# Taking the norm of the sample's block apart: scaling ahead of the first products, transposes between gate's and up's

## The chip, the core and the metric

The kernel runs on one core of a Trainium2 chip. A core has a matrix engine (TensorE, in the profile PE, with its weight loads as PEld) and three engines for element-wise work: VectorE (DVE), ScalarE (ACT) and GpSimd (POOL). SyncE (SP) issues most transfers. Each engine works its instructions off in the order in which they were put into its queue; an instruction that waits holds up all that stand behind it. The metric is the device time of one execution in microseconds. The kernel before takes 1778.29 us, the median of three runs (1778.0 to 1786.5).

## The reference

One inference step of a small two-layer network for two groups of tokens: a prompt of 512 rows and a sample of 8 x 16 = 128 rows, each row 1024 wide, in float32. Layer 0 has a mixer of two kinds of attention, layer 1 a banded softmax attention; after each mixer comes the same feed-forward part (FFN):

```python
def _rmsnorm(x, g):
    y = xf * lax.rsqrt(jnp.mean(xf * xf, axis=-1, keepdims=True) + EPS)
    return (y * g.astype(jnp.float32)).astype(x.dtype)

def _swiglu(h, wg, wu, wd):
    return (jax.nn.silu(h @ wg) * (h @ wu)) @ wd

xp = xp + _swiglu(_rmsnorm(xp, norm_ffn_g[layer]), w_ffn_gate[layer], w_ffn_up[layer], w_ffn_down[layer])
xs = xs + _swiglu(_rmsnorm(xs, norm_ffn_g[layer]), w_ffn_gate[layer], w_ffn_up[layer], w_ffn_down[layer])
```

The hidden width of the FFN is 2816. The change touches only how the norm of the sample's rows is fitted into the start of each of the two FFNs.

## The kernel before

Prompt and sample are handled together as 640 rows in five blocks of 128; block 4 is the sample. Weights in float32 are split into a high part (`wh`, a rounded copy made by ACT, line 289) and a low part (`wl`, the rest, made by DVE, line 290), and each product is three matmuls: high by high, high by low, low by high (lines 692 to 694). There are four buffers each for `wh` and `wl`, so splits run up to four products ahead.

**The norm of a block** is `norm_block` (line 247). `rstd_of` (line 230) forms the reciprocal root: ACT squares both halves of the rows and sums them (`sqj`, line 235), DVE adds (`rv`, 240), ACT takes logarithm and exponential (`rr`, 241 and 242), DVE does a correction step (`ra`, 243, and `rr`, 244). Then each half of the rows is scaled into a tile `h` (line 252), the first half by DVE, the second by POOL; PE transposes it in four pieces into a bank of PSUM (`tp`, line 255); and ACT and DVE in turn bring the eight pieces into the transposed input `fT`, multiplied by the norm's weight (lines 261 and 263).

**The FFN** (`ffn`, line 738) takes the columns of the 640 rows in two halves of 320: the first is prompt only, the second holds the rest of the prompt and the sample. Its weights gate and up are worked through in pairs of 128 columns; each pair of columns of one matrix is an entry of `mats` with four functions. `part(0)` and `part(1)` are the plain products with the first and the second half of the rows; each makes four products of 12 matmuls, 48 in all, into two tiles `pb`. `head`, `body` and `tail` are a form with seven products in place of eight (tiles `py`, `px`, `pq`), which needs sums of weights (`sw`, made by POOL at line 699) and sums of the input (`comb`, DVE at line 657, tiles `xs`). `block` splits a part of the input into high (`xb`, `xt`, ACT at line 664) and low (DVE at line 665). The blocks `b11` and `b21` cover the first half of the rows, `b12` and `b22` the second; `t1` to `t4` are those of the sums.

The first entries of gate and up are done by plain products, since the sample's rows come last: they are complete only when `out_sample` has added its product to them (line 626), right ahead of the FFN. The order in the program is: blocks b11 and b21, `part(0)` of gate, `part(0)` of up, the norm of block 4, blocks b12 and b22, `part(1)` of gate, `part(1)` of up, `head` of the next pair, the sums and blocks t1 to t4, and then the pairs' bodies:

```python
block("b11")
block("b21")
part(0)
last_norm(mats[1][3](0))
block("b12", gt_)
```

`part(0)` returns its last matmul. What `last_norm` gets is the last matmul of up's first half; the transposes are bound to be issued behind it (`tc.issue_after`, line 253).

The queues' order is made by a planner that goes by the program's order (an earlier statement has priority), by when operands are ready in its own estimate, and by the free buffers of each tag. The tag `ws` has six buffers; the tiles `sqj`, `h`, the results `sg` of gate and `up` of up, and `xs` share it. The plain products' tiles `pb` and the transposes' `tp` share five banks of PSUM.

Of the kernel before, what the change touches and what calls it, by code (L numbers as in the profile page):

```python
# [13 lines left out]
ALU = mybir.AluOpType  # L14
PSUM = bass.MemoryType.PSUM

P = 128
# [38 lines left out]
def kernel(  # L56
# [8 lines left out]
    nc = tc.nc  # L65
# [27 lines left out]
    @contextmanager  # L93
    def ffn_pools():
        with tc.tile_pool(name="ffn", bufs=1, reuse_waits="tile") as m:
            pools["stage"] = m
            with tc.tile_pool(name="pf", bufs=5, space=PSUM, reuse_waits="tile") as a:
                banks.update(za=a, zb=a)
                yield

    def tagged(tag, bufs, where="all"):
        def f(shape, name, dt=F32):
            return pools[where].tile(shape, dt, tag=tag, bufs=bufs, name=name)
        return f
# [5 lines left out]
    ws = tagged("ws", NWS)  # L110
# [108 lines left out]
        fill=0.0, base=DS - 1, channel_multiplier=-1,  # L219
    )  # L220

    xs_flat = x_sample.rearrange("b t d -> (b t) d")

    def x_rows(src_p, src_s, b):
        return src_p[0, b * P:(b + 1) * P, :] if b < 4 else src_s
# [4 lines left out]
    def rstd_of(xt, sb=None):  # L230

        ss = small.tile([P, 2], F32, tag="ss", name="ss")
        for i in range(2):
            j = (sb or ws)([P, 512], "sqj")
            nc.scalar.activation(j, xt[i], AF.Square, scale=1.0 / 32.0, accum_out=ss[:, i:i + 1])
        v = small.tile([P, 1], F32, tag="rv", name="rv")
        r = small.tile([P, 1], F32, tag="rr", name="rr")
        a = small.tile([P, 1], F32, tag="ra", name="ra")
        V = nc.vector
        V.tensor_scalar(v, ss[:, 0:1], ss[:, 1:2], EPS, op0=ALU.add, op1=ALU.add)  # L240
        nc.scalar.activation(r, v, AF.Ln)
        last_exp[:] = [nc.scalar.activation(r, r, AF.Exp, scale=-0.5)]
        V.tensor_scalar(a, r, r, v, op0=ALU.mult, op1=ALU.mult)
        V.tensor_scalar(r, a, -3.0, r, op0=ALU.add, op1=ALU.mult)
        return r

    def norm_block(xt, gi, hT, b, sb=None, bank=None, after=None):
        r = rstd_of(xt, sb)
        for i in range(2):
            tp = (bank or za)([P, 4, P], "tp")  # L250
            h = (sb or ws)([P, 512], "h")
            scaled = (nc.vector, nc.gpsimd)[i].tensor_scalar(h, xt[i], r, -0.5, op0=ALU.mult, op1=ALU.mult)
            with tc.issue_after(after.ins) if after else nullcontext():
                for j in range(4):
                    nc.tensor.transpose(tp[:, j, :], h[:, j * P:(j + 1) * P], ident)
            for j in range(4):
                c = 4 * i + j
                if len(hT) == 4:
                    d = hT[c // 2][:, c % 2, b * P:(b + 1) * P]
                    if j % 2:  # L260
                        nc.vector.tensor_scalar(d, tp[:, j, :], gm[:, gi, c:c + 1], None, op0=ALU.mult)
                    else:
                        nc.scalar.activation(d, tp[:, j, :], AF.Copy, scale=gm[:, gi, c:c + 1])
                    continue
                H = hT[c][:, 0, b * P:(b + 1) * P]
                L = hT[c][:, 1, b * P:(b + 1) * P]
                g = gm[:, gi, c:c + 1]
                nc.scalar.activation(H, tp[:, j, :], AF.Copy, scale=g)
                nc.vector.scalar_tensor_tensor(
                    L, tp[:, j, :], g, H.bitcast(F32), op0=ALU.mult, op1=ALU.subtract)  # L270
        return scaled

    def new_hT(nm):
        return [t5([P, 2, NT], f"{nm}{c}", F32R) for c in range(8)]

    def new_fT(nm):

        return [t5([P, 2, NT], f"{nm}{c}") for c in range(4)]
# [459 lines left out]
    def ffn(l, xt, fT, after, last_norm):  # L738
        X, comb, block = operand(fT)
        c0, silu = 0, []  # L740
        for gi, G in enumerate(GROUPS):
            gT, mats = [], []
            for c in range(c0, c0 + G, 2):
                gt = [(t5 if gi % 2 == 0 and c == c0 else gt_)([P, 2, NT], "gT", F32R) for _ in range(2)]
                gT += gt
                sg = [ws([P, 2, 320], "sg") for _ in range(2)]

                def out_g(m, n, a, b, sg=sg, done=[0, 0]):
                    if b is None:
                        nc.scalar.copy(sg[m][:, n, :], a)  # L750
                    else:
                        nc.vector.tensor_add(sg[m][:, n, :], a, b)
                    done[m] += 1
                    if done[m] == 2:

                        with tc.issue_after(last_exp[0].ins):
                            silu.append(nc.scalar.activation(sg[m], sg[m], AF.Silu))

                def out_u(m, n, a, b, sg=sg, gt=gt, up=[None, None]):
                    if up[m] is None:  # L760
                        up[m] = ws([P, 2, 320], "up")
                    if b is None:
                        nc.scalar.copy(up[m][:, n, :], a)
                    else:
                        nc.vector.tensor_add(up[m][:, n, :], a, b)
                    if b is None and n == 0:
                        return
                    g = gt[m].rearrange("p i (n t) -> p i n t", n=2)
                    for i in range(2) if b is None else (n,):
                        s = sg[m][:, i, :]  # L770
                        nc.vector.tensor_mul(s, s, up[m][:, i, :])
                        nc.scalar.copy(g[:, 0, i, :], s)
                        nc.vector.tensor_sub(g[:, 1, i, :], s, g[:, 0, i, :].bitcast(F32))
                for w, o in ((w_ffn_gate, out_g), (w_ffn_up, out_u)):
                    mats.append(fast_pair(w[l], c * P, X, o))
            for i, (head, body, tail, part) in enumerate(mats):
                if gi == 0 and i == 1:
                    continue
                if gi == 0 and i == 0:


                    block("b11")
                    block("b21")
                    part(0)
                    last_norm(mats[1][3](0))
                    block("b12", gt_)
                    block("b22")
                    part(1)
                    mats[1][3](1)
                    mats[2][0]()  # L790
                    comb("t3", "b22", "b12")
                    block("t3")
                    comb("t1", "b12", "b11")
                    comb("t2", "b22", "t1")
                    block("t2")
                    block("t1")
                    comb("t4", "b21", "t2")
                    block("t4")
                    continue
                if gi or i > 2:  # L800
                    head()
                if i > 2 * (gi == 0):
                    mats[i - 1][2]()
                body()
            mats[-1][2]()
            if gi == len(GROUPS) - 1:
                with tc.issue_after(silu[-1].ins):
                    nc.scalar.preload_act_table_set(LOGSET)
            for half in range(2):
                last = half == 1 and gi == len(GROUPS) - 1  # L810

                def ev(b, ps):
                    nc.vector.tensor_add(xt[b][half], xt[b][half], ps)
                proj_as(l, w_ffn_down[l][c0 * P:(c0 + G) * P, :], 512 * half, 512, gT, ev,
                        tail=TAIL if last else 1, after=after if last else None)
            c0 += G
# [11 lines left out]
    hT = new_hT("hTa")  # L828
# [266 lines left out]
    for t in ORDER.split():  # L1095
        step(t)
    hT = new_fT("fT0")
    xt = mixer_end(w_out_ab[0], oT, oS, lambda b: x_rows(x_prompt, xs_flat, b), 1, hT, a_sample,
                   [FIRST + 99500 + 1000 * t for t in WHEN[0]])
# [9 lines left out]
        last_scaled[:] = [norm_block(xt[b], 2, hT2, b)]  # L1109
    stack.close()  # L1110
    with ffn_pools():
        ffn(0, xt, hT, after0, lambda mm: norm_block(xt[4], 1, hT, 4, after=mm))
    hT = hT2


# [53 lines left out]
    for half in range(2):  # L1169
# [7 lines left out]
        for p in range(p0 + 1, p0 + 4):  # L1177
            c_attend(p, *c_pair(p))

    hT = new_fT("fT1")  # L1180
    xt = mixer_end(w_out_c[0], oT, oS, lambda b: xd[b], 3, hT, lambda: (mixer_banks(*BANKS[2]), [c_sample(h) for h in range(2)]),
                   [FIRST + 299500 + 1000 * t for t in WHEN[1]])
# [11 lines left out]
        nc.sync.dma_start(dst, y)  # L1194
    stack.close()
    with ffn_pools():
        ffn(1, xt, hT, after1, lambda mm: norm_block(xt[4], 3, hT, 4, after=mm))


# [37 lines left out]
```

## Time and profile before

| | |
|---|---|
| median of three runs | 1778.29 us |
| profiled execution: its own time | 1781.72 us |
| profiled execution: span | 1780.0 us |
| granted TensorE clock, mean | 0.979 |
| busy: PE / PEld | 95% / 86% |
| busy: DVE / ACT / POOL | 62% / 46% / 18% |
| chain that ended last: PE / DVE / ACT | 82% / 11% / 3% |

The profile is of one execution. The page gives busy time per engine, the span in 40 slices, the chain of waits that ended last, and groups of instructions by line. A row of a timeline gives the start in us from the span's start, the duration, the engine, the line, the operation, `out<-in`, the shape, how many instructions were merged, and in brackets how long the engine had been idle and which instruction ended that. A row of the table of stretches gives, for each stretch, its length, each engine's busy time with the number of instructions, the granted clock, and the transfers' share and rate. FFN 0 begins at about 440 us, FFN 1 at about 1321 us.

### The profile page before, as it was taken

The page shows a single profiled execution, that of the slowest core. Times are in us where ns is not written, and L with a number is a line of the kernel's source. Part 1 is how long each engine was busy: PE and PEld are TensorE (multiplying, and loading weights), DVE is VectorE, ACT ScalarE, POOL GpSimd, SP SyncE. Part 2 cuts the span into 40 slices and gives each one's busy share as a digit, 9 for nine tenths or more (in the row PEclk, how much of TensorE's full clock was granted, in tenths as well). Part 3 has the DMA queues.
Part 4 walks back from the last instruction along what each step waited for, and adds up shares of the span by engine and source line. Part 5 has one row for each costly group of instructions (what it writes and reads, how often), then busy time and mean ns, then how long its engine had stood idle before and what let it go on. Part 6 is the DMA issues. An engine that isn't in the chain of part 4 may idle for free.

```text
span 1780.0 us, 31737 instructions
## 1 busy us (share of the span) xinstructions
PE 1697.9 (95%) x12520; PEld 1522.9 (86%) x12520; DVE 1108.4 (62%) x2237; ACT 812.0 (46%) x1805; POOL 317.7 (18%) x339
## 2 busy tenths in 40 slices
PE   7999999998889999999999999999787999999997
PEld 7898997896788998989898889888567889899896
DVE  6466586765684765856555654755647837658465
ACT  6454435455552543534454433534536525335253
POOL 2000000000241413414110000001104224043130
PEclk9999998999899999999999999999998999999999
DMA  5311131574122222222343233368822313222212
GB/s 144 97 56 49 56 97 54 186 244 155 59 77 90 71 96 71 73 95 70 122 134 99 83 96 108 116 211 300 311 98 62 105 60 95 83 83 73 93 60 83
DMA packets 157173, 192.09 MB, mean 108 GB/s; under 512 B 12976, under 2 KB 109248, under 8 KB 157024
## 3 DMA queue, kind: packets, MB, share of 16 engines
q1 hardware_dynamic: 153440, 178.40, 30.8%
q0 software_dynamic: 3584, 11.67, 2.1%
q8 instruction: 98, 1.61, 0.4%
q14 instruction: 51, 0.42, 0.1%
HBM read 175.75 MB, written 14.29 MB: 107 GB/s over the span
## 4 chain that ended last, share of the span: by engine, by line
PE 82%; DVE 11%; ACT 3%; issue 2%; DMA 2%; SPq 0%; DVEq 0%; ACTq 0%
PE pn L323 6%; PE pn L325 6%; PE pn L324 6%; PE pw L304 5%; PE pw L305 5%; PE pw L306 5%; DVE wl L290 3%; PE px L692 3%; PE px L693 3%; PE px L694 3%; PE kttp L535 2%; PE py L694 2%; PE pm L356 2%; PE pm L359 2%; PE pm L358 2%
## 5 line engine op out<-in xcount | busy, mean ns | idle before, releaser
L290 DVE TENSOR_TENSOR wl<-raw,wh 128x512 fp32r<-128x512 f32 (+1 forms) x370 | 289.0, 788 | 251.0 <-ACT wh L289 248.5
L289 ACT CAST wh<-raw 128x512 fp32r<-128x512 f32 (+1 forms) x370 | 227.8, 618 | 377.7 <-PE pn L325 163.4
L699 POOL TENSOR_TENSOR sw<-raw 128x512 f32<-128x512 f32 x80 | 128.5, 1610 | 533.2 <-DMA raw<-in_w_ffn_gate_dram 298.2
L324 PE MATMUL pn<-wl,gT 128*128 128x512 f32 x440 | 171.2, 389 | 0.0
L289 ACT CAST wh<-sw 128x512 fp32r<-128x512 f32 x160 | 99.4, 621 | 154.9 <-PE px L693 64.4
L325 PE MATMUL pn<-wh,gT 128*128 128x512 f32 x440 | 169.3, 389 | 0.0
L323 PE MATMUL pn<-wh,gT 128*128 128x512 f32 x440 | 166.8, 389 | 0.0
L290 DVE TENSOR_TENSOR wl<-sw,wh 128x512 fp32r<-128x512 f32 x160 | 120.7, 758 | 52.6 <-ACT wh L289 41.4
L694 PE MATMUL py<-xb,wl 128*128 128x320 f32 x320 | 100.6, 314 | 9.2 <-DVE wl L290 9.2
L694 PE MATMUL pq<-xt,wl 128*128 128x320 f32 x320 | 98.8, 310 | 4.0 <-DVE wl L290 4.0
L692 PE MATMUL pq<-xt,wh 128*128 128x320 f32 x320 | 99.1, 310 | 2.2 <-ACT wh L289 2.2
L692 PE MATMUL px<-xt,wh 128*128 128x320 f32 x320 | 98.9, 309 | 0.0
L693 PE MATMUL pq<-xt,wh 128*128 128x320 f32 x320 | 98.9, 309 | 0.0
L693 PE MATMUL px<-xt,wh 128*128 128x320 f32 x320 | 98.9, 309 | 0.0
L694 PE MATMUL px<-xt,wl 128*128 128x320 f32 x320 | 98.9, 309 | 0.0
L693 PE MATMUL py<-xb,wh 128*128 128x320 f32 x320 | 98.8, 309 | 0.0
L692 PE MATMUL py<-xb,wh 128*128 128x320 f32 x320 | 98.8, 309 | 0.0
L325 PEld LDWEIGHTS pn<-wh,gT 128*128 128x128 f32 x440 | 82.6, 188 | 16.9
L324 PEld LDWEIGHTS pn<-wl,gT 128*128 128x128 f32 x440 | 82.6, 188 | 16.9
L323 PEld LDWEIGHTS pn<-wh,gT 128*128 128x128 f32 x440 | 82.3, 188 | 16.6
L304 PE MATMUL pw<-hTa,wh 128*128 128x320 f32 (+1 forms) x272 | 89.9, 331 | 0.0
L305 PE MATMUL pw<-hTa,wh 128*128 128x320 f32 (+1 forms) x272 | 88.9, 327 | 0.0
(329 smaller groups left out, 4721.5 us busy)
## 6 DMA issues: line engine op xcount, KB each, us to landing
raw<-in_w_ffn_gate_dram SPq DMA_DIRECT2D x44, 512.0 KB, 3.8
raw<-in_w_ffn_up_dram SPq DMA_DIRECT2D x44, 512.0 KB, 3.7
raw<-in_w_ffn_down_dram SPq DMA_DIRECT2D x44, 512.0 KB, 3.3
kr<-in_cache_c_k_dram SPq DMA_DIRECT2D x64, 256.0 KB, 5.4
vr<-in_cache_c_v_dram SPq DMA_DIRECT2D x16, 1024.0 KB, 7.0
raw<-in_w_in_ab_dram SPq DMA_DIRECT2D x24, 512.0 KB, 3.8
raw<-in_w_qkv_c_dram SPq DMA_DIRECT2D x24, 512.0 KB, 3.8
vr<-in_cache_a_v_dram SPq DMA_DIRECT2D x8, 1024.0 KB, 5.6
```

Of the source, the lines that this page charges most:

```text
L289: nc.scalar.copy(H, rawv)
L290: nc.vector.tensor_sub(L, rawv, H.bitcast(F32))
L304: MM(ps[i], lhsT=H[:, k % 4, :], rhs=hT[k][:, 0, s], start=(k == 0), stop=False)
L305: MM(ps[i], lhsT=H[:, k % 4, :], rhs=hT[k][:, 1, s], start=False, stop=False)
L306: MM(ps[i], lhsT=L[:, k % 4, :], rhs=hT[k][:, 0, s], start=False, stop=(k == 7))
L323: MM(ps[b], lhsT=lhs[k][:, 0, bs], rhs=H, start=(k == 0), stop=False)
L324: MM(ps[b], lhsT=lhs[k][:, 0, bs], rhs=L, start=False, stop=False)
L325: MM(ps[b], lhsT=lhs[k][:, 1, bs], rhs=H, start=False, stop=(k == K - 1))
L692: MM(ps, lhsT=H[:, k, :], rhs=X[x][0][k], start=(first and k == 0), stop=False, **f)
L693: MM(ps, lhsT=H[:, k, :], rhs=X[x][1][k], start=False, stop=False, **f)
L694: last = MM(ps, lhsT=L[:, k, :], rhs=X[x][0][k], start=False, stop=(k == 3), **f)
L699: nc.gpsimd.tensor_tensor(t, a, b, op=op)
```

## The change

The norm is taken apart into two functions. `norm_rows` does the reciprocal root and both scalings and returns the two tiles `h`; `norm_columns` does the transposes and what follows them. `norm_block`, which all other blocks use, calls one after the other; the only difference there is that both scalings stand ahead of the first transposes.

In each FFN, `norm_rows` of block 4 now stands ahead of blocks b11 and b21, that is ahead of all plain products, and both its scalings are on DVE (`ROWS`). `norm_columns` of block 4 stands behind gate's `part(0)`, and its transposes are bound to be issued behind that part's last matmul; up's `part(0)` follows the transposes. The sums, the number of instructions and the products are the same; one scaling per FFN goes from POOL to DVE.

```diff
+    ROWS = (nc.vector, nc.vector)
...
-    def norm_block(xt, gi, hT, b, sb=None, bank=None, after=None):
+    def norm_rows(xt, sb=None, engines=None):
+
         r = rstd_of(xt, sb)
+        hs = []
         for i in range(2):
+            h = (sb or ws)([P, 512], "h")
+            scaled = (engines or (nc.vector, nc.gpsimd))[i].tensor_scalar(
+                h, xt[i], r, -0.5, op0=ALU.mult, op1=ALU.mult)
+            hs.append(h)
+        return hs, scaled
+
+    def norm_block(xt, gi, hT, b, sb=None, bank=None):
+        hs, scaled = norm_rows(xt, sb)
+        norm_columns(hs, gi, hT, b, bank)
+        return scaled
+
+    def norm_columns(hs, gi, hT, b, bank=None, after=None):
+
+        for i, h in enumerate(hs):
             tp = (bank or za)([P, 4, P], "tp")
-            h = (sb or ws)([P, 512], "h")
-            scaled = (nc.vector, nc.gpsimd)[i].tensor_scalar(h, xt[i], r, -0.5, op0=ALU.mult, op1=ALU.mult)
             with tc.issue_after(after.ins) if after else nullcontext():
                 for j in range(4):
                     nc.tensor.transpose(tp[:, j, :], h[:, j * P:(j + 1) * P], ident)
...
+                    rows = last_norm[0]()
                     block("b11")
                     block("b21")
-                    part(0)
-                    last_norm(mats[1][3](0))
+                    last_norm[1](rows, part(0))
+                    mats[1][3](0)
                     block("b12", gt_)
                     block("b22")
...
-        ffn(0, xt, hT, after0, lambda mm: norm_block(xt[4], 1, hT, 4, after=mm))
+        ffn(0, xt, hT, after0, (lambda: norm_rows(xt[4], engines=ROWS)[0],
+                              lambda rows, mm: norm_columns(rows, 1, hT, 4, after=mm)))
...
-        ffn(1, xt, hT, after1, lambda mm: norm_block(xt[4], 3, hT, 4, after=mm))
+        ffn(1, xt, hT, after1, (lambda: norm_rows(xt[4], engines=ROWS)[0],
+                              lambda rows, mm: norm_columns(rows, 3, hT, 4, after=mm)))
```

More of the change, by code (lines that the diff above doesn't have):

```diff
@@ L270, in norm_block @@
                     L, tp[:, j, :], g, H.bitcast(F32), op0=ALU.mult, op1=ALU.subtract)
-        return scaled
     def new_hT(nm):
```

## The prediction

> **What bounds the kernel now.** I read the page first: busy shares, the span in slices, the chain of waits.
>
> ```profile
> span 1780.0 us, 31737 instructions
> PE 1697.9 (95%) x12520; PEld 1522.9 (86%) x12520; DVE 1108.4 (62%) x2237; ACT 812.0 (46%) x1805; POOL 317.7 (18%) x339
> PEclk9999998999899999999999999999998999999999
> PE 82%; DVE 11%; ACT 3%; issue 2%; DMA 2%; SPq 0%; DVEq 0%; ACTq 0%
> ```
>
> TensorE sets the time, so a gain must be time in which PE stands or runs at a low clock. The granted clock dips in slices 7, 11 and 31 (of 44.5 us each); the last two are where the two FFNs begin, and the change touches only these. There I read PE's timeline, FFN 0 and then FFN 1 (start, duration, instruction, idle time before it and what ended it):
>
> ```profile
> 454.30 0.31 PE L694 MATMUL pb<-xb,wl 128*128 128x320 f32 x1
> 459.57 1.94 PE L255 MATMUL tp<-ident,h 128*128 128x128 f32 x8 [4.95 <-DVE h L252]
> 462.77 0.90 PE L692 MATMUL pb<-xb,wh 128*128 128x320 f32 x2 [1.26 <-ACT xb L664]
> 465.59 0.63 PE L693 MATMUL pb<-xb,wh 128*128 128x320 f32 x1 [1.92 <-DVE xb L665]
> ...
> 466.29 0.47 PE L692 MATMUL pb<-xb,wh 128*128 128x320 f32 x1
> 466.55 0.47 PE L693 MATMUL pb<-xb,wh 128*128 128x320 f32 x1
> ...
> 478.06 0.31 PE L692 MATMUL pb<-xb,wh 128*128 128x320 f32 x1
> ...
> 481.14 0.31 PE L692 MATMUL py<-xb,wh 128*128 128x320 f32 x1
> ...
> 1335.36 0.31 PE L694 MATMUL pb<-xb,wl 128*128 128x320 f32 x1
> ...
> 1361.98 0.31 PE L692 MATMUL py<-xb,wh 128*128 128x320 f32 x1
> ```
>
> 454.30 is the last product of up's first half, 481.14 the first of the next pair. Between them lie three waits, 4.95 + 1.26 + 1.92 = 8.13 us, then products that start 0.26 us apart (466.29 to 466.55) instead of 0.147 (21 steps from 478.06 to 481.14, 3.08 us). The waits follow one chain, seen on ACT, DVE and POOL:
>
> ```profile
> 439.21 0.69 DVE L626 TENSOR_TENSOR x<-x,ps 128x512 f32<-128x512 f32 x1 [6.18 <-PE ps L625]
> 454.50 0.62 ACT L289 CAST wh<-raw 128x512 fp32r<-128x512 f32 x1 [1.14 <-PE pb L693]
> 455.03 0.42 ACT L763 COPY up<-pb 128x320 f32<-128x320 f32 x1
> 455.34 0.63 ACT L235 ACTIVATE sqj<-x 128x512 f32<-128x512 f32 x1
> 458.06 1.36 DVE L252 TENSOR_SCALAR h<-x,rr 128x512 f32<-128x512 f32 x1
> 459.12 0.86 POOL L252 TENSOR_SCALAR h<-x,rr 128x512 f32<-128x512 f32 x1
> 460.69 0.37 ACT L263 ACTIVATE fT<-tp,gm 128x128 f32<-128x128 f32 x1 [3.30 <-PE tp L255]
> ```
>
> The sample's rows are complete at 439.90, but their squares run at 455.34, right behind up's last copy, although ACT had stood idle (1.14 us ahead of 454.50 alone). So their place in the program's order holds them back, not their data; I read it as the working tiles of one tag being handed out in program order. The diff changes just that order.
>
> **What full speed would be.** The eight transposes took 0.79 us at full clock, from 439.01 to the product at 439.80:
>
> ```profile
> 439.01 1.04 PE L255 MATMUL tp<-ident,h 128*128 128x128 f32 x8
> 439.80 0.39 PE L692 MATMUL pb<-xb,wh 128*128 128x320 f32 x1
> ...
> 441.49 0.31 PE L694 MATMUL pb<-xb,wl 128*128 128x320 f32 x1
> 441.80 0.41 PE L692 MATMUL pb<-xb,wh 128*128 128x320 f32 x1
> ```
>
> From the last first-half product to the next pair PE needs 0.15 + 0.79 + 96 x 0.147 = 15.05 us (two second halves of 48 products). FFN 0 takes 481.14 - 454.30 = 26.84, 11.79 too many; FFN 1 takes 1361.98 - 1335.36 = 26.62, 11.57 too many. That is 23.4 us, the most this change can recover there.
>
> **Part by part.**
>
> *Rows ahead of the plain products.* The squares, logarithm, exponential and three small DVE operations come first, and both scalings go to DVE; nothing is added or dropped. In FFN 1 the second half of x is ready at about 1322.3 and ACT has nothing until 1323.23:
>
> ```profile
> 1321.63 0.69 DVE L626 TENSOR_TENSOR x<-x,ps 128x512 f32<-128x512 f32 x1 [1.39 <-PE ps L625]
> 1323.23 0.62 ACT L289 CAST wh<-raw 128x512 fp32r<-128x512 f32 x1 [4.60 <-PE pb L693]
> ```
>
> The chain from first square to first transpose was 459.57 - 455.34 = 4.23 us. It ends at about 1326.5, and gate's first half ends 48 x 0.147 = 7.1 us ahead of up's last product at 1335.36, at 1328.3. Cost 0; cover 1.8 us, and what the rows are later than that, up's whole half on PE would wait, for it is queued behind the transposes. In FFN 0 x is ready at 439.90 and the squares meet the weight casts, which stand behind them in ACT's queue and for which PE waits:
>
> ```profile
> 439.65 1.59 ACT L263 ACTIVATE fT<-tp,gm 128x128 f32<-128x128 f32 x4 [9.71 <-PE tp L255]
> 441.14 2.17 ACT L289 CAST wh<-raw 128x512 fp32r<-128x512 f32 x4
> ```
>
> PE already waits for the first of these casts (the next product starts 441.80, 0.31 after 441.49 instead of 0.147). One square (0.63) with its readout in front of them delays it by 0.7; the other square can go at 433. The bounds are 0 and 3.6 (the chain's 4.23 less one square). I take 1.0, near the single square. The second scaling costs DVE about 0.5 instead of POOL 0.86; DVE idles through the first halves (next fence), so 0, uncovered 0.5 per FFN.
>
> *Transposes between gate and up.* The same eight; what is queued behind them on PE is now up's first half, which has its weights (four split buffers run ahead). What follows them (eight evictions, the blocks b12 and b22) now has up's 48 products as cover, 7.1 us. It took 465.59 - 460.69 = 4.9 us to the first low part. In that cover:
>
> ```profile
> 439.60:454.60 15.00, 15.00 (x101) 14.27 (x98) 8.35 (x15) 8.31 (x18) 0.00 (x0) 1.00 0.00 1
> 446.90:454.60 7.70, 7.70 (x53) 7.45 (x51) 2.91 (x5) 3.23 (x7) 0.00 (x0) 1.00 0.00 0
> 454.60:469.40 14.80, 6.67 (x25) 5.88 (x25) 9.93 (x15) 6.32 (x16) 6.36 (x5) 0.65 0.24 71
> 469.40:481.10 11.70, 11.70 (x82) 11.70 (x81) 7.38 (x12) 9.62 (x17) 0.00 (x0) 1.00 0.30 91
> 481.10:500.00 18.90, 15.45 (x102) 14.67 (x100) 18.90 (x25) 12.16 (x23) 15.01 (x4) 1.00 0.18 55
> 500.00:520.00 20.00, 18.09 (x121) 17.83 (x122) 18.43 (x28) 9.51 (x19) 10.39 (x8) 1.00 0.25 81
> ```
>
> (columns: length, then busy time of PE, weight load, DVE, ACT, POOL; granted clock; transfers). Over up's first half DVE is busy 2.91 of 7.70 us, ACT 3.23. Undisturbed the blocks come 2 us early; with all of ACT's 3.23 ahead they come 1.1 late, with a little from DVE 1.5. I take 0.5 per FFN. Without the waits the clock need not fall (0.65 in the third row): the 0.12 us on each of some 14 products and the slower transposes go too, already in the 11.79.
>
> *Work that filled the stall.* DVE did 9.93 us in the third row. 6.65 of it fits into DVE's idle time in the first (15.00 - 8.35), the other 3.3 into the fourth (4.3 idle). If it doesn't, it lands in the pairs' products, where DVE is busy 18.90 of 18.90 us and PE loses 3.45. Bounds 0 and 3.3 per FFN; I take 1.0, nearer nothing, since the burst keeps its place behind the gate's second half: the t3 blocks start right behind the gT casts,
>
> ```profile
> 477.93 0.46 ACT L772 CAST gT<-sg 128x320 fp32r<-128x320 f32 x1
> 478.29 1.35 ACT L664 CAST xt<-xs 128x640 fp32r<-128x640 f32 x2
> ```
>
> and those wait for the gate's result, which comes earlier by the same time. Loads of the next weights follow the splits of the same products and move along; no queue is passed that wasn't before.
>
> *Sum.* 23.4 - 1.0 - 2 x 0.5 - 2 x 1.0 = 19.4 us. The profiled execution took 1781.72 (span 1780.0), so 1762.3 on its own scale; that execution lies 3.4 above the median 1778.29, which gives 1778.3 - 19.4 = 1759. With all bounds at their worst, 23.4 - 3.6 - 3.0 - 6.6 = 10.2, it is 1768; with none, 1755.
>
> A rule that speaks against the change: POOL's weight sums were quick beside a half-idle DVE, and one took 9.82 us beside a full one:
>
> ```profile
> 457.88 1.26 POOL L699 TENSOR_TENSOR sw<-raw 128x512 f32<-128x512 f32 x1 [25.54 <-DVE ra L243]
> 463.13 1.72 POOL L699 TENSOR_TENSOR sw<-raw,sw 128x512 f32<-128x512 f32 x1
> 483.77 9.82 POOL L699 TENSOR_TENSOR sw<-raw 128x512 f32<-128x512 f32 x1 [18.92 <-DVE wl L290]
> ```
>
> The Trainium skill, SBUF — State Buffer, section "SBUF: two separate sides", says that DVE and GpSimd share one port pair, held for a whole instruction while the other is blocked. By that rule the first four sums (three of some 1.3 us, one of 1.7) could hold DVE up 5.5 us per FFN in gate's second half. The trace agrees that the two hinder each other: DVE's scaling took 1.36 us beside the sum at 457.88, so the 9.93 holds a part of this already. Against 4.3 idle the rule would cost 1.2 more per FFN, and the time would be 1761.
>
> **Rivals.**
>
> *DVE pays it back.* If the 9.93 us can't be done earlier because DVE's order ties them behind splits that wait for PE, the full burst is late: 23.4 - 2.0 - 19.9 = 1.5, so 1777; half of it, 1767. For it: 18.90 of 18.90. Against: 6.65 us idle in the first halves.
>
> *The pairs gain as well.* PE loses 3.45 + 1.91 = 5.4 us per FFN in the last two rows. If part of DVE's burst comes before the pairs, half goes: 5.4 more in all, 1753.5. Against: the t3 blocks' place.
>
> *It doesn't do what it says.* If the rows still come late, PE stands before the transposes after gate's half: the 4.95 and the slow clock (14 x 0.12 and the transposes' 1.94 - 1.04, some 2.6) stay, 11.7 - 7.6 = 4.1 per FFN is won, 1770. Against: x is complete in time.
>
> *Slower: POOL's sums starve.* The first four sums now run while DVE does b12, b22 and t3 without the pause that PE's stall gave. They start at about 460 (457.88 now, later by the transposes' 0.8 and FFN 0's 1.0); the fourth is needed at 478 (the pair starts at 481.1 - 9.7, and 48 products, 7.1 us, come first). At 9.82 each they end at 499, 21 late, less 9.7 won: 11.5 slower per FFN, 1801. It turns slower than before above (478 + 9.7 - 460)/4 = 6.9 us each. Against: even beside the saturated DVE four took 15.01 us together, 3.8 each.
>
> **How the numbers follow.** Forecast 1759, 0.69. DVE pays half 0.08, all 0.06. Pairs gain too 0.06. Doesn't do it 0.06. POOL starves 0.05. Half a per cent, about what a measurement of this kernel can tell from no change, is 8.9 us, so faster means below 1769.4: 0.69 + 0.08 + 0.06 = 0.83; within: 0.06 + 0.06 = 0.12; slower 0.05. The forecast's own range is 1755 to 1768; 1752 to 1770 takes in half the payback and most of the pairs' gain, 8 in 10.
>
> **What would show it.** In each FFN: squares right behind the addition to x, no wait of PE ahead of the eight transposes, these between gate's and up's first halves, granted clock near 1 through the second halves, and 15 to 17 us from the last product of gate's first half plus up's 48 to the next pair. Wrong would be: a wait of over 1.5 us at the first product of gate's second half, more than 5.4 us lost in the two stretches after the pairs begin, or sums on POOL above 5 us before the first pair.

## The result and the profile after

The changed kernel takes 1759.4 us (median of four runs, 1754.15 to 1762.34), the kernel before beside it 1779.05 us (median of four, 1778.0 to 1786.5). The ratio is 0.9871 with a 95% interval of 0.9844 to 0.9898: 1.3% faster, 19.65 us between the medians. The profiled execution took 1759.97 us. The page of the changed kernel, its span, busy times and granted clock in slices:

```profile
span 1758.2 us, 31735 instructions
PE 1692.0 (96%) x12520; PEld 1515.7 (86%) x12520; DVE 1114.7 (63%) x2239; ACT 811.4 (46%) x1805; POOL 314.5 (18%) x337
PEclk9999998899999999999999999999999999999999
```

The span is 21.8 us shorter. The two dips of the clock at the starts of the FFNs are gone; the two slices that still show 8, the seventh as before and now the eighth, lie in the first mixer. PE's timeline shows both starts (start, duration, instruction, idle time before it and what ended it); lines after the change stand some 14 further down in the code, so that the transposes are L270 and the products L706 to L708:

```profile
438.89 0.39 PE L706 MATMUL pb<-xb,wh 128*128 128x320 f32 x1
...
441.40 0.41 PE L706 MATMUL pb<-xb,wh 128*128 128x320 f32 x1 [0.50 <-DVE rr L245]
...
442.92 0.41 PE L708 MATMUL pb<-xb,wl 128*128 128x320 f32 x1 [0.44 <-DVE wl L304]
...
447.58 0.31 PE L708 MATMUL pb<-xb,wl 128*128 128x320 f32 x1
447.72 1.04 PE L270 MATMUL tp<-ident,h 128*128 128x128 f32 x8
...
469.71 0.31 PE L706 MATMUL py<-xb,wh 128*128 128x320 f32 x1
...
1308.97 0.71 PE L706 MATMUL pb<-xb,wh 128*128 128x320 f32 x1
...
1316.41 1.03 PE L270 MATMUL tp<-ident,h 128*128 128x128 f32 x8
...
1338.40 0.31 PE L706 MATMUL py<-xb,wh 128*128 128x320 f32 x1
```

The eight transposes stand between gate's half and up's half and nothing waits ahead of them, nor from there to the next pair. For the account of the whole span three more landmarks are needed: of the kernel before, the first product of FFN 1 and in both FFNs the first addition of the down product to x,

```profile
555.38 0.69 DVE L813 TENSOR_TENSOR x<-x,pn 128x512 f32<-128x512 f32 x1 [2.68 <-PE pn L325]
...
1321.03 0.71 PE L692 MATMUL pb<-xb,wh 128*128 128x320 f32 x1
...
1436.26 0.69 DVE L813 TENSOR_TENSOR x<-x,pn 128x512 f32<-128x512 f32 x1 [2.68 <-PE pn L325]
```

and the same two additions of the changed kernel:

```profile
544.22 0.69 DVE L828 TENSOR_TENSOR x<-x,pn 128x512 f32<-128x512 f32 x1 [2.68 <-PE pn L339]
...
1413.44 0.69 DVE L828 TENSOR_TENSOR x<-x,pn 128x512 f32<-128x512 f32 x1 [2.68 <-PE pn L339]
```

| stretch (us) | before | after | gain |
|---|---|---|---|
| up to FFN 0's first product | 439.80 | 438.89 | 0.91 |
| FFN 0: first product to the pair's first (`py`) | 41.34 | 30.82 | 10.52 |
| FFN 0: pair to first addition of the down product | 74.24 | 74.51 | -0.27 |
| from there to FFN 1's first product | 765.65 | 764.75 | 0.90 |
| FFN 1: first product to the pair's first | 40.95 | 29.43 | 11.52 |
| FFN 1: pair to first addition | 74.28 | 75.04 | -0.76 |
| the rest | 343.74 | 344.76 | -1.02 |
| span | 1780.0 | 1758.2 | 21.8 |

The two starts give 22.0 us; behind them 1.0 is lost again in the pairs. A second profiled execution of the changed kernel (below) has the same two starts to the hundredth, 30.82 and 29.43, but takes 75.24 and 76.07 behind them, so that 2.8 are lost there: the starts repeat, the losses behind them vary from execution to execution. The other three stretches, in which the change does next to nothing, add 0.8 together, and are of the size by which executions of one kernel differ.

### The profile page after: what moved, and what is told of

Read it like the earlier page. It is cut to its first block, busy times and chain, and to the rows that moved or that the text cites. A ratio compares the mean times of both kernels' runs of the same rounds, so it can differ in the third digit from the quotient of the medians.

```text
span 1758.2 us, 31735 instructions
## 1 busy us (share of the span) xinstructions
PE 1692.0 (96%) x12520; PEld 1515.7 (86%) x12520; DVE 1114.7 (63%) x2239; ACT 811.4 (46%) x1805; POOL 314.5 (18%) x337
## 3 DMA queue, kind: packets, MB, share of 16 engines
q0 software_dynamic: 3584, 11.67, 2.1%
## 4 chain that ended last, share of the span: by engine, by line
PE 83%; DVE 10%; ACT 3%; DMA 2%; issue 2%; SPq 0%; DVEq 0%; ACTq 0%
PE pn L337 6%; PE pn L339 6%; PE pn L338 6%; PE pw L318 5%; PE pw L319 5%; PE pw L320 5%; DVE wl L304 4%; PE px L707 3%; PE px L706 3%; PE px L708 3%; PE kttp L549 2%; PE py L708 2%; PE pm L370 2%; PE pm L373 2%; PE pm L372 2%
## 5 line engine op out<-in xcount | busy, mean ns | idle before, releaser
L304 DVE TENSOR_TENSOR wl<-raw,wh 128x512 fp32r<-128x512 f32 (+1 forms) x370 | 294.8, 805 | 233.5 <-ACT wh L303 231.1
L708 PE MATMUL py<-xb,wl 128*128 128x320 f32 x320 | 101.2, 316 | 10.0 <-DVE wl L304 9.9
L708 PE MATMUL pq<-xt,wl 128*128 128x320 f32 x320 | 98.9, 310 | 1.9 <-DVE wl L304 1.8
L706 PE MATMUL pq<-xt,wh 128*128 128x320 f32 x320 | 99.1, 310 | 0.9 <-ACT wh L303 0.9
L706 PE MATMUL px<-xt,wh 128*128 128x320 f32 x320 | 98.9, 309 | 0.0
L706 PE MATMUL py<-xb,wh 128*128 128x320 f32 x320 | 98.9, 309 | 0.0
L708 PE MATMUL px<-xt,wl 128*128 128x320 f32 x320 | 98.8, 309 | 0.0
L318 PE MATMUL pw<-hTa,wh 128*128 128x320 f32 (+1 forms) x272 | 89.5, 329 | 0.0
L320 PE MATMUL pw<-hTa,wl 128*128 128x320 f32 (+1 forms) x272 | 88.5, 325 | 0.0
```

Of the source, the lines that this page charges most:

```text
L304: nc.vector.tensor_sub(L, rawv, H.bitcast(F32))
L318: MM(ps[i], lhsT=H[:, k % 4, :], rhs=hT[k][:, 0, s], start=(k == 0), stop=False)
L320: MM(ps[i], lhsT=L[:, k % 4, :], rhs=hT[k][:, 0, s], start=False, stop=(k == 7))
L706: MM(ps, lhsT=H[:, k, :], rhs=X[x][0][k], start=(first and k == 0), stop=False, **f)
L708: last = MM(ps, lhsT=L[:, k, :], rhs=X[x][0][k], start=False, stop=(k == 3), **f)
```

## The experiments

The theory was the prediction's: PE stood because the rows came late by their place in the program, and because nothing covered the way from the transposes to the first blocks b12; the two parts of the change remove one each. The rivals were that one part does it all, that DVE or POOL give the gain back, and that what waits is something else than the order of the buffers. The first four kernels ran on one chip beside 23 runs of the kernel before (median 1783.31 us), the last four on another beside 9 (1782.43). "The stage" below is the time from an FFN's first product to the first addition of its down product: 115.58 and 115.23 us before, 105.33 and 104.47 after (106.06 and 105.50 in the second execution of the changed kernel, so the stages of one kernel differ by up to 1 us).

### Only the rows early

The rows are made ahead of the products as in the change; the transposes go back behind up's half.

```diff
                     rows = last_norm[0]()
                     block("b11")
                     block("b21")
-                    last_norm[1](rows, part(0))
-                    mats[1][3](0)
+                    part(0)
+                    last_norm[1](rows, mats[1][3](0))
```

> The changed kernel, but with the transposes back behind up's first half: only the rows (squares to scalings) stand ahead of the plain products. My theory: the first wait (4.95 us per FFN) goes, for the scaled rows are ready some 8 us before PE reaches the transposes; the two waits behind them stay, because evictions and blocks have no products over them. First eviction to first low part was 4.9 us, of which PE covers some 0.5, so about 4.4 us per FFN are lost, and the clock may hold. Gain 11.7 - 4.4 per FFN, less 1.2 at FFN 0's start and some 2 later on: 11 to 12 us, 1766 to 1768. Rival (the rows alone do it, the transposes' place is worth nothing): as the changed kernel, 1759. Rival (the place of the transposes is what counts): no gain, 1778.

Measured: 1771.64 us (median of 8), ratio 0.994 (0.9921 to 0.9959); stages 110.91 and 108.83. PE's timeline of FFN 0:

```profile
455.49 1.04 PE L270 MATMUL tp<-ident,h 128*128 128x128 f32 x8
458.22 0.56 PE L706 MATMUL pb<-xb,wh 128*128 128x320 f32 x2 [1.69 <-ACT xb L678]
459.32 0.64 PE L707 MATMUL pb<-xb,wh 128*128 128x320 f32 x1 [0.54 <-DVE xb L679]
...
463.69 0.41 PE L707 MATMUL pb<-xb,wh 128*128 128x320 f32 x1 [1.03 <-DVE xb L679]
```

The wait ahead of the transposes is gone, those behind them stay: 3.26 us together in FFN 0, where some 4.4 were expected. The rows alone are worth 4.67 + 6.40 = 11.1 us of stage, and 11.7 us between the medians, as expected; the expected time, 1766 to 1768, was missed because the kernel before took 1783.31 us on this chip and not 1778.

### Only the transposes early

The transposes stand behind gate's half, but the rows are made there too.

```diff
-                    rows = last_norm[0]()
                     block("b11")
                     block("b21")
-                    last_norm[1](rows, part(0))
+                    mm = part(0)
+                    rows = last_norm[0]()
+                    last_norm[1](rows, mm)
                     mats[1][3](0)
```

> The changed kernel, but the rows are computed only behind gate's first half, straight before the transposes: the transposes' new place alone. My theory: PE now stands about 5 us ahead of the transposes as in the kernel before, with up's half queued behind them, the clock falls, but the evictions and blocks are covered by up's half, so no wait before the second halves. Gain 11.7 - 5.0 - 2.6 = 4.1 per FFN, 8 us, less some 2 later on: 1770 to 1772. Rival (the chain is hidden behind gate's casts anyway): as the changed kernel, 1759. Rival (PE's wait grows, since up's half can no longer cover anything): 1778 or more.

Measured: 1775.64 us (median of 10), ratio 0.996 (0.9942 to 0.9977); stages 110.55 and 111.79. The mirror image on PE's timeline, in FFN 0 and FFN 1:

```profile
454.37 1.58 PE L270 MATMUL tp<-ident,h 128*128 128x128 f32 x8 [3.99 <-DVE h L254]
...
1329.83 1.94 PE L270 MATMUL tp<-ident,h 128*128 128x128 f32 x8 [4.08 <-DVE h L254]
```

The wait ahead of the transposes is back at 4 us, with slow transposes behind it, and there are no waits between them and the pair. This part alone is worth 5.03 + 3.44 = 8.5 us of stage, and 7.7 us between the medians, against 6 to 8 expected. The two parts give 11.1 + 8.5 = 19.6, the whole change 10.25 + 10.76 = 21.0, or 19.25 in its second execution: neither does it alone, and they add up within what executions differ by.

### What held the squares back

The prediction read the late squares as the working tiles of one tag being handed out in program order. Here the kernel before keeps its whole order; only the tiles `sqj` and `h` of this one norm come from another tag.

```diff
-        ffn(0, xt, hT, after0, lambda mm: norm_block(xt[4], 1, hT, 4, after=mm))
+        ffn(0, xt, hT, after0, lambda mm: norm_block(xt[4], 1, hT, 4, t5, after=mm))
...
-        ffn(1, xt, hT, after1, lambda mm: norm_block(xt[4], 3, hT, 4, after=mm))
+        ffn(1, xt, hT, after1, lambda mm: norm_block(xt[4], 3, hT, 4, t5, after=mm))
```

> The kernel before, program order unchanged; only the working tiles of the sample's norm (squares and scaled rows) are taken from another tag's buffers than those of the results of gate and up. My theory of why the squares came late: buffers of one tag are handed out in program order, so the squares wait for up's last copy to take its buffer. Then here the squares run right behind the addition to x (at about 440 and 1323) without any reordering of the program, the first wait of 4.95 us goes and the two behind it stay: as with the rows alone, 1766 to 1768. Rival (the place in the program itself holds them back, as lower priority): squares at 455 and 1336 as before, 1778.

Measured: 1775.53 us (median of 10), ratio 0.9961 (0.9941 to 0.998); stages 110.56 and 108.90. ACT's and PE's timelines of FFN 0 (the lines are those of the kernel before):

```profile
437.56 0.63 ACT L235 ACTIVATE sqj<-x 128x512 f32<-128x512 f32 x1
...
452.90 1.03 PE L255 MATMUL tp<-ident,h 128*128 128x128 f32 x8
455.62 0.56 PE L692 MATMUL pb<-xb,wh 128*128 128x320 f32 x2 [1.69 <-ACT xb L664]
456.79 0.41 PE L693 MATMUL pb<-xb,wh 128*128 128x320 f32 x1 [0.61 <-DVE xb L665]
...
461.17 0.41 PE L693 MATMUL pb<-xb,wh 128*128 128x320 f32 x1 [2.35 <-DVE xb L665]
```

The square shown, of the half of x that is ready last (at 437.53), runs at 437.56, ahead of the weight casts, where both squares stood at 455.34 and behind. So it was neither the data nor the place in the program by itself, but the tag that the tiles share with gate's and up's results. The changed kernel keeps the tag and moves the place, this one keeps the place and changes the tag, and the squares come early in both: that fits buffers of one tag that go out in program order. The stages gain 5.02 + 6.33 = 11.4 us, the same as the rows' move. The timed gain, 0.2 to 0.6%, is 3.6 to 10.5 us, less than the profiled execution shows (its span is 1766.9, 13.1 below that of before) and less than the 10 to 12 expected. The profiled execution was the fastest of the ten, at a mean granted clock of 0.985; the other nine had 0.978 to 0.982. Where they lost it no trace shows.

### The second scaling back on POOL

```diff
-    ROWS = (nc.vector, nc.vector)
+    ROWS = (nc.vector, nc.gpsimd)
```

> The changed kernel, but the second scaling stays on POOL. My theory: DVE saves 0.44 us where PE waits for DVE's low parts at the start of FFN 0 (0.44 us there), POOL's 0.83 us is covered by gate's half: 1759, less at most 0.5. Rival (the move to DVE is what frees POOL or the rows): slower by 1 us or more per FFN, 1761 or more.

Measured: 1761.11 us (median of 4), ratio 0.9885 (0.985 to 0.992). PE's timeline, gate's first half in FFN 0, from the one wait left to the transposes:

```profile
439.68 0.39 PE L706 MATMUL pb<-xb,wh 128*128 128x320 f32 x1
...
442.19 0.41 PE L706 MATMUL pb<-xb,wh 128*128 128x320 f32 x1 [0.51 <-DVE rr L245]
...
448.10 1.03 PE L270 MATMUL tp<-ident,h 128*128 128x128 f32 x8
```

Gate's half takes 448.10 - 439.68 = 8.42 us instead of 447.72 - 438.89 = 8.83; the wait of 0.44 for a low part is gone. Such a gain is far below what the times can show, and the medians cannot be told apart. The stages, 107.61 and 105.20 us, do not show it either: behind the pair FFN 0 took 77.20 us in this execution, against 74.51 and 75.24 in the two of the changed kernel, at a granted clock of 0.91 from 490 to 510 us where both of those had 1.00 in the same part. So the 0.44 is shown at its place only, and the rival, 1 us or more lost per FFN, is not excluded by these figures.

### The changed kernel once more

It ran again beside the last three kernels.

> The changed kernel again, unchanged, as the measure for the kernels run beside it. Expected 20 to 24 us below the kernel before on the same chip.

Measured: 1764.19 us (median of 4, 1761.05 to 1768.71), ratio 0.9901 (0.9877 to 0.9925); stages 106.06 and 105.50, with the same two waits at FFN 0's start, 0.50 and 0.44 us. It is 18.2 us below the kernel before beside it, a little less than the 20 to 24 expected.

### Can the sums' blocks come earlier?

The prediction kept the pairs as they were because the blocks t3 stand behind the casts of gate's result. The changed kernel shows the two next to each other on ACT:

```profile
467.65 0.46 ACT L786 CAST gT<-sg 128x320 fp32r<-128x320 f32 x1 [1.64 <-DVE sg L785]
468.02 1.35 ACT L678 CAST xt<-xs 128x640 fp32r<-128x640 f32 x2
```

The first `gT` and t3 share a tag, and b12 shares another with the later `gT`; in this kernel the two change places.

```diff
-                gt = [(t5 if gi % 2 == 0 and c == c0 else gt_)([P, 2, NT], "gT", F32R) for _ in range(2)]
+                gt = [(t5 if gi == 2 and c == c0 else gt_)([P, 2, NT], "gT", F32R) for _ in range(2)]
...
-                    block("b12", gt_)
+                    block("b12")
```

> The changed kernel with two tags swapped at an FFN's start: block b12 goes into the general buffers, the first results gT into the stage's own. Nothing else moves in the program. It tells what limits the first pairs, where PE still loses some 4.6 us per FFN. My theory: the t3 blocks queue behind the gT casts only because both draw on one tag; freed of it they run about 10 us earlier, beside the second halves, where DVE idles 3.2 of 16.0 us; what DVE does there it need not do in the pairs, where it is busy all the time. Gain 1 to 3 us per FFN, 2 to 6 below the changed kernel. Rival (DVE's work as a whole binds from the transposes to the pairs' end): no gain, within 1 us of the changed kernel. Rival (the earlier burst delays the splits that the second halves wait for): slower by 1 to 3 us per FFN.

Measured: 1762.79 us (median of 4), ratio 0.9889 (0.986 to 0.9919), not to be told from the changed kernel. The first t3 cast on ACT, and two stretches of FFN 0 from the transposes at 449.53 on (length, then busy time of PE, weight load, DVE, ACT and POOL; clock; transfers):

```profile
458.35 0.73 ACT L678 CAST xt<-xs 128x640 fp32r<-128x640 f32 x1
...
449.50:471.50 22.00, 22.00 (x154) 21.99 (x153) 19.88 (x29) 16.25 (x32) 8.34 (x4) 1.00 0.30 91
471.50:490.00 18.50, 15.22 (x98) 14.02 (x97) 18.46 (x24) 11.75 (x23) 6.37 (x4) 1.00 0.14 38
```

Counted from the transposes t3 comes 11.5 us earlier (458.35 - 449.53 = 8.82, in the changed kernel 468.02 - 447.72 = 20.30), by the tags alone as with the squares. Yet from the transposes to the first addition FFN 0 takes 546.11 - 449.53 = 96.58 us, against 542.86 - 445.63 = 97.23 in the changed kernel beside it and 544.22 - 447.72 = 96.50 in its first execution: nothing gained that can be told. DVE is busy 19.88 of 22.00 us ahead of the pair and 18.46 of 18.50 behind it. That fits the rival that DVE's work as a whole binds, not the order of its parts: an earlier t3 puts off other work of DVE that PE also waits for. FFN 0's start even lost, by a wait on PE of about 2.2 us in this kernel and the two below where the changed one has 0.50:

```profile
442.39 0.42 PE L706 MATMUL pb<-xb,wh 128*128 128x320 f32 x1 [2.19 <-ACT wh L303]
```

The cast had itself waited 1.57 us for gate's load; why the load comes later with the tags changed was not followed.

Two more kernels went on from there: t2's sums from another tag,

```diff
-                    comb("t2", "b22", "t1")
+                    comb("t2", "b22", "t1", t5)
```

> As the run with the tags swapped, and the sums for t2 also take general buffers in place of those shared with the results of gate and up, so that t2 and t1 need not wait for these either. My theory: more of the burst moves into the second halves, up to DVE's 3.2 idle us per FFN in all; 3 to 6 us below the changed kernel. Rival (DVE binds as a whole): no better than the swap alone. Rival (splits come late): PE waits in the second halves.

and beside that the sums of t3 and t1 moved from DVE to POOL.

```diff
-                    comb("t3", "b22", "b12")
+                    comb("t3", "b22", "b12", eng=nc.gpsimd)
                     block("t3")
-                    comb("t1", "b12", "b11")
+                    comb("t1", "b12", "b11", eng=nc.gpsimd)
```

> As the last, with the sums for t3 and t1 (four of 128x640 per FFN, 0.8 us each on DVE) made by POOL, which idles until the weight sums at about 460. My theory: DVE is relieved by 3.2 us per FFN, PE's loss in the pairs falls by as much at most: 2 to 6 us below the kernel without this. Rival (POOL's sums and DVE hinder each other): POOL takes 2 us or more per sum, delays the weight sums and blocks, no gain or 2 to 4 us slower.

Measured: 1768.2 us (median of 4), ratio 0.9919 (0.9899 to 0.994), and 1773.7 us (median of 6), ratio 0.9954 (0.9937 to 0.9971). Both expectations failed. The first is 4.0 us above the changed kernel beside it, with ranges that overlap; the second is 9.5 above it, with none of its runs as fast as the slowest there. Part of that is a new wait, on POOL's, DVE's and PE's timelines of FFN 0:

```profile
467.63 2.12 POOL L671 TENSOR_TENSOR xs<-fT 128x640 f32<-128x640 f32 x1
...
468.27 2.03 DVE L304 TENSOR_TENSOR wl<-raw,wh 128x512 fp32r<-128x512 f32 x1
...
470.36 0.41 PE L708 MATMUL pb<-xb,wl 128*128 128x320 f32 x1 [1.95 <-DVE wl L304]
```

The four sums moved to POOL, of 1.59 to 2.12 us each, stand in POOL's queue among the sums of weights, and PE waits 1.95 us for a low part in the middle of the second halves, where the changed kernel has no wait. The rows show how: the low part, mostly 0.69 us long, took 2.03 beside POOL's sum of 2.12, ended at 470.30, 0.55 after that sum, and PE goes on at 470.36. So POOL's sums and DVE do hinder each other, as the rival had it. The queues' order changes with the move too: in the kernel without it a low part there takes 1.79 us beside a sum of weights and PE waits only 0.21, so how much of the loss each of the two costs was not told apart. None of the kernels is clearly faster than the changed one.

## Why the prediction was right, point by point

*The time.* Forecast 1759, measured 1759.4; the sum 19.4 us against 19.65 between the medians and 21.8 between the two spans. The runs of before differ by 8.5 us among themselves, so the agreement to half a microsecond is luck; the stages in the traces say more.

*Rows at no cost in FFN 1.* Held. DVE's scalings there, and for a later point its last low parts of the blocks in FFN 0:

```profile
452.77 1.55 DVE L679 TENSOR_TENSOR xb<-fT,xb 128x640 fp32r<-128x640 f32 x2
...
1312.33 0.88 DVE L254 TENSOR_SCALAR h<-x,rr 128x512 f32<-128x512 f32 x2
```

The scalings end at 1313.21 and the transposes start at 1316.41, a cover of 3.2 us where 1.8 was reckoned.

*1.0 us at FFN 0's start.* The size held: gate's first half takes 8.83 us where 48 x 0.147 = 7.06 would do, 1.77 too many, while the two halves of before took 0.54 too many. That is 1.2, and the second execution has the same 8.83. The place was only half right. ACT's and DVE's timelines of the changed kernel:

```profile
432.15 0.63 ACT L236 ACTIVATE sqj<-x 128x512 f32<-128x512 f32 x1 [3.12 <-DVE x L640]
...
439.02 0.63 ACT L236 ACTIVATE sqj<-x 128x512 f32<-128x512 f32 x1
...
440.74 2.17 ACT L303 CAST wh<-raw 128x512 fp32r<-128x512 f32 x4
...
441.38 0.88 DVE L254 TENSOR_SCALAR h<-x,rr 128x512 f32<-128x512 f32 x2
442.18 2.49 DVE L304 TENSOR_TENSOR wl<-raw,wh 128x512 fp32r<-128x512 f32 x4
```

One square stands in front of the casts and the other runs at 432, as reckoned; against the FFN's first product the casts are 0.5 later (440.74 - 438.89 = 1.85, before 441.14 - 439.80 = 1.34). But the two scalings stand in front of the low parts on DVE, and a part of the cost is there: PE waits 0.50 for the casts' side and 0.44 for `wl`. (The row of the first wait names `rr`, which ended at 441.34; the product reads `wh`, whose first cast was under way from 440.74 to about 441.4.) The step by which the second scaling on DVE costs 0, since DVE idles through the first halves, was right for the sum of the stretch and wrong for this place in the queue; with one scaling on POOL the 0.44 is gone there.

*0.5 us per FFN at gate's second half.* Did not come. The last low part of b12 and b22 is done at 452.77 + 1.55 = 454.32, 6.6 us after the transposes start, and gate's second half starts 0.79 + 7.06 = 7.85 us after them. So the blocks were 1.2 us early: ACT's 3.23 us of other work did not delay them by as much as was allowed for, the bound "2 us early" was the nearer one, and 1.0 of the gain was left out.

*1.0 us per FFN of displaced work of DVE.* Right in kind; its size is not settled. By the account it is 0.27 and 0.76 us, in the second execution 75.24 - 74.24 = 1.00 and 76.07 - 74.28 = 1.79. The table of stretches of the changed kernel (columns as above), to be read beside that of the prediction:

```profile
438.70:453.70 15.00, 14.05 (x95) 13.30 (x94) 11.67 (x26) 11.46 (x28) 0.00 (x0) 1.00 0.01 2
453.70:469.70 16.00, 16.00 (x111) 16.00 (x110) 12.84 (x17) 10.46 (x19) 5.68 (x4) 1.00 0.41 113
469.70:489.00 19.30, 16.41 (x102) 14.62 (x100) 19.30 (x25) 12.55 (x25) 14.29 (x4) 1.00 0.19 53
489.00:509.00 20.00, 18.34 (x124) 18.00 (x123) 19.43 (x29) 10.04 (x22) 10.77 (x8) 1.00 0.31 96
```

From the FFN's start to the pair DVE did 8.35 + 9.93 + 7.38 = 25.66 us of work before (first, third and fourth row there) and does 11.67 + 12.84 = 24.51 now, in 10.5 us less time. So nearly the whole burst found room, 1.2 us was left for the pairs, and PE is never idle in the second row, at full clock. Behind the pair PE stands 2.89 + 1.66 = 4.55 us in the last two rows, 0.8 less than before; since the way to the down product takes 0.27 longer all the same, some 1.1 is lost later. That fits the displaced work, but its way was not followed further.

*The sum again.* With the measured sizes it is 23.4 - 1.2 - 0 - 1.0 = 21.2 us, against 21.0 for the two stages (10.25 + 10.76); with the second execution's 2.8 in the last place 19.4, against 19.25. So only the term at gate's second half is clearly too large, and what is lost behind the pairs varies by more than that.

*The rivals.* That the change does not do what it says, and that DVE pays half or all back, fell with these rows. That the pairs gain too fell with t3's place, which held (467.65 and 468.02), and the experiment that moved t3 shows that its place would not have been enough. POOL's sums did not starve ahead of the pair:

```profile
459.59 1.30 POOL L713 TENSOR_TENSOR sw<-raw 128x512 f32<-128x512 f32 x1 [28.16 <-DMA raw<-in_w_ffn_gate_dram]
...
463.12 1.43 POOL L713 TENSOR_TENSOR sw<-sw,raw 128x512 f32<-128x512 f32 x1
464.63 1.64 POOL L713 TENSOR_TENSOR sw<-raw,sw 128x512 f32<-128x512 f32 x1
473.49 10.92 POOL L713 TENSOR_TENSOR sw<-raw 128x512 f32<-128x512 f32 x2 [7.23 <-DVE wl L304]
```

The first and the last of the four took 1.30 and 1.64 us with DVE busy 12.84 of 16.00, and two took 10.92 us behind the pair with DVE busy 19.30 of 19.30. I read it as DVE's gaps letting POOL through, of which there were enough ahead of the pair; no run took that apart.

The price that the prediction set against the change, DVE held up by these sums, shows on DVE's timeline, beside the last two of the four:

```profile
463.31 1.79 DVE L304 TENSOR_TENSOR wl<-raw,wh 128x512 fp32r<-128x512 f32 x1
...
465.02 1.59 DVE L787 TENSOR_TENSOR gT<-sg,gT 128x320 fp32r<-128x320 f32 x1
```

Such operations take 0.69 and 0.49 us where no sum runs. Here they end at 465.10 and 466.61, about half a microsecond after the sums beside them (464.55 and 466.27). With two more (1.28 for 0.69, 0.80 for 0.48) DVE lost 3.1 us to the four sums, where the prediction allowed 5.5; in the kernel before it had lost 2.3 to them in the same way, inside the 9.93 (the scaling 1.36 for 0.49, and three operations from 462.52 to 466.27). The Trainium skill's rule (SBUF — State Buffer, "SBUF: two separate sides"), by which the one that comes second waits for the other's whole instruction, agrees with these rows. Its price in the prediction, 1.2 us more per FFN and 1761, does not show in the second halves: DVE had 3.16 us idle besides, and PE has no wait from 447.72 to 469.71. What it adds behind the pair cannot be told from the other displaced work, and the times are too near each other to decide it.

*What would show it.* From the last product of gate's half to the pair, without up's 48 products, 469.71 - 447.58 - 7.06 = 15.07 us: within the 15 to 17 named, at its low end since no wait is left. None of the signs against it came.

## What to carry to other kernels

When work runs late although its data were there and its engine idle, look for what it shares with others: here one tag's buffers, handed out in program order, held squares back from 439.90, when their data were there, to 455.34, and a tag of its own or an earlier place in the program frees them alike. Put the dependent chain of a late operand (norm, transposes, blocks) beside independent matrix work at both of its links, not one; each link is worth its own wait. Gains below 5 us do not show in a median of this kernel, so read them from the stage in the trace, look further down for what it pays back, and take a second execution: the starts repeated to the hundredth here, what lay behind them only to about 1 us per FFN.

## What had not been expected

Runs of one kernel differ by more than the change's smaller terms: the changed kernel from 1754.15 to 1768.71 us over eight runs, at a mean granted clock of 0.980 to 0.988. The two go together: 1754.15 us came with 0.988 and 1768.71 with 0.980, and of the 23 runs of the kernel before the fastest, 1774.49, with 0.981 and the slowest, 1788.7, with 0.974.

The granted clock does not follow from the waits alone. With only the rows early, and with only the other tag, PE has nearly the same waits behind the transposes (1.69 and 0.54; 1.69 and 0.61). In the first the clock fell, in these stretches of the two kernels (columns as above), first of the rows-only kernel,

```profile
458.90:462.30 3.40, 2.98 (x11) 2.98 (x12) 3.40 (x5) 1.40 (x3) 2.02 (x2) 0.51 0.39 131
```

and then of the kernel with the other tag:

```profile
456.30:461.00 4.70, 2.03 (x12) 1.76 (x12) 4.70 (x5) 1.46 (x3) 3.73 (x3) 1.00 0.27 89
```

The Trainium skill (TensorE: Matmul & The Clock Gate, "What's actually happening") says that activity is watched in windows of some 3.4 us that run freely, whatever the kernel does; the 3.4 us at 0.51 and their absence behind the same waits agree with it (the 3.4 us on either side had 0.99 and 1.00). The low clock cost nothing in FFN 0: from the transposes to the end of the last wait the one took 463.69 - 455.49 = 8.20 us, the other 461.17 - 452.90 = 8.27, since the slow products only filled time in which PE waits for DVE's low part (1.03 instead of 2.35). There DVE and not PE set the pace, so the low clock was no loss.
